# First products and gelus of 16 of 128 expert blocks moved behind the step that builds the routing weights

## The chip, the cores and the metric

The kernel runs on one core of one Trainium2 chip. The metric is device time in microseconds (us) of one execution, as the median of several runs. The engines are PE (TensorE, matrix products), DVE (VectorE), ACT (ScalarE), POOL (GpSimd) and SP (SyncE, which only issues transfers here). Each engine takes its instructions strictly in the order in which the program lists them.

## What is computed

One encoder layer runs on two groups of tokens, a prompt of 256 and a sample of 1024. The part that matters is its last one, a mixture of 16384 experts (PEER). For each token, 8 heads pick 16 experts each. A picked expert has a row of `peer_u` and a row of `peer_v`:

```
act = gelu(einsum('td,thkd->thk', zt, u)) * g      # zt: the normalised token, u: rows of peer_u, g: softmax of the picks
out = einsum('thk,thkd->td', act, ve)              # ve: the same experts' rows of peer_v
```

The result is added to the token and normalised once more.

## The kernel before, in words

A token's experts are worked out in one of two ways. In blocks of 128 tokens that **gather**, the picked rows are fetched one slot at a time by indirect transfers that POOL issues: `ug` (rows of `peer_u`, 512 KB for 128 tokens) is multiplied and summed by DVE at L940, and `vg` (rows of `peer_v`) goes either to PE at L976 (`v_steps`) or to DVE at L996 (`v_slots`, the last two blocks). Both share one ring of seven buffers. Six token blocks gather: two of the prompt and four of the sample. The other 512 tokens of the sample are **dense**: all 16384 experts are computed for them, in 128 expert blocks of 128 experts.

For the dense tokens the order of the work is this. `merge` picks experts; at its end `half` and `finish_picks` work out, for each of four dense chunks of 128 tokens, the picks' codes (DVE with some ACT work) and store them in `codes` (L911). `weights` then builds the routing weight of each expert for each token: `cs` loads the codes, PE makes indicators (L1034), ACT and DVE turn them into `ol` and `oh`, PE multiplies these (L1053), ACT copies the result to `gs` (L1054), and after every eighth of its 128 groups `gs` is stored in DRAM as `gd`. Last, `dense` takes the 128 expert blocks in groups of four. `first(b)` loads a block of `uT` (512 KB), splits it in a high and a low part (`uh` on ACT, `ul` on DVE), multiplies it with the tokens `zt` in 24 matmuls (L140 to L142 with `zth`, `ztl`), applies the gelu (ACT, L1080), multiplies with the weights `g`, loaded from `gd` for four blocks at a time, and splits the product into `ah` and `al`. `second(g)` loads eight pieces of `peer_v` (256 KB each), splits them into `vh` and `vl`, and does 96 matmuls for the four blocks.

The gathers of the sample's blocks run beside all of this: those of the first block beside the end of `merge`, those of the others beside `weights` and `dense`. In `v_steps` every fourth gathered `vg` is followed on PE by eight matmuls of L976, one **slot group** below; between two of them POOL issues four `vg` and four `ug`. A token block has 32 slot groups. The scheduler fixes the order of every engine when the program is built, so a slot group has a fixed place among PE's other matmuls. A block of 24 first products is called a **first block** below.

The pools that matter: `uraw`, `uh` and `ul` have two buffers each, `ge` two. Until the change, `weights` has five PSUM banks and `dense` three for its first products.

Of the kernel before, what the change touches and what calls it, by code (L numbers as in the profile page):

```python
# [12 lines left out]
F32 = mybir.dt.float32  # L13
# [5 lines left out]
AF = mybir.ActivationFunctionType  # L19
# [5 lines left out]
P = 128  # L25
D = 1024
KD = D // P
# [23 lines left out]
def encoder(ctx, tc, I, O, dbg=None):  # L51
    nc = tc.nc
# [3 lines left out]
    dram = ctx.enter_context(tc.tile_pool(name="dram", bufs=1, space=DRAM))  # L56
# [56 lines left out]
    qd_ = dram.tile([MH, 96, SS], F32, name="qd_")  # L113
    ND = 512
    gd = dram.tile([ND // TC, P, P * TC], F32, name="gd")
    codes = dram.tile([ND // P, 2, P, 4, P], BF16, name="codes")


    def split(pool, src, shape, name, bufs=None, eng=None):
        kw = {} if bufs is None else {"bufs": bufs}  # L120
        hi = pool.tile(shape, F32R, name=name + "h", tag=name + "h", **kw)
        lo = pool.tile(shape, F32R, name=name + "l", tag=name + "l", **kw)
        nc.scalar.copy(hi, src)  # L123
        (eng or nc.vector).tensor_tensor(lo, src, hi.bitcast(F32), op=OP.subtract)  # L124
        return hi, lo
# [10 lines left out]
    def mm(out, w, x, start, stop):  # L136
        if len(w) == 1:
            nc.tensor.matmul(out, w[0], x[0], start=start, stop=stop)  # L138
            return
        nc.tensor.matmul(out, w[0], x[0], start=start, stop=False)  # L140
        nc.tensor.matmul(out, w[0], x[1], start=False, stop=False)  # L141
        nc.tensor.matmul(out, w[1], x[0], start=False, stop=stop)  # L142
# [11 lines left out]
    def put(dst, src):  # L154

        if len(dst) == 1:
            nc.scalar.copy(dst[0], src)
        else:
            nc.scalar.copy(dst[0], src)
            nc.vector.tensor_tensor(dst[1], src, dst[0].bitcast(F32), op=OP.subtract)  # L160
# [764 lines left out]
    def ring(name):  # L925
        return pe_.tile([P, D], F32, name=name, tag="ring", bufs=RING)
# [75 lines left out]
    def final_gain():  # L1002
        gfin = ring("gfin")
        nc.sync.dma_start(gfin, I["norm_final"].partition_broadcast(P))
        return gfin

    def finish(y, sq, tt, gfin=None):
        gfin = final_gain() if gfin is None else gfin
        ss = pe_.tile([P, 1], F32, name="fss", tag="fss")
        nc.scalar.activation(out=sq, in_=y, func=AF.Square, accum_out=ss)  # L1010
        rs = pe_.tile([P, 1], F32, name="frs", tag="frs")
        rsqrt_small(pe_, rs, ss, 1.0 / D, [P, 1], "fin")
        nc.vector.scalar_tensor_tensor(out=y, in0=y, scalar=rs[:, 0:1], in1=gfin, op0=OP.mult, op1=OP.mult)
        nc.gpsimd.dma_start(O["y"][tt:tt + P], y)
# [43 lines left out]
    def load_split(pool, src, shape, name, bufs):  # L1058
        raw = pool.tile(shape, F32, name=name + "raw", tag=name + "raw", bufs=2)
        nc.sync.dma_start(raw, src)  # L1060
        return split(pool, raw, shape, name, bufs)

    def dense(routes, zt, acc, dp, up, bankS, bankV):

        nt = len(routes)
        nch = ND // TC
        held = {}
        a_of = {}

        def first(b):  # L1070
            u = load_split(up, I["uT"][b], [P, KD, P], "u", 2)
            if b % HB == 0:
                held["g"] = dp.tile([P, nch, HB, TC], F32, name="g", tag="g", bufs=2)
                nc.scalar.dma_start(held["g"].rearrange("p c h t -> p c (h t)"),
                                    gd[:, :, b * TC:(b + HB) * TC].rearrange("c p x -> p c x"))
            pm = bankS()
            for k in range(KD):
                mm(pm, [x[:, k] for x in u], [x[:, k] for x in zt], k == 0, k == KD - 1)
            ge = dp.tile([P, ND], F32, name="ge", tag="ge", bufs=2)
            nc.scalar.activation(out=ge, in_=pm, func=AF.Gelu)  # L1080
            gev = ge.rearrange("p (c t) -> p c t", t=TC)
            nc.vector.tensor_tensor(gev, gev, held["g"][:, :, b % HB], op=OP.mult)
            a_of[b] = (dp.tile([P, ND], F32R, name="ah", tag="ah", bufs=GE + 1),
                       dp.tile([P, ND], F32R, name="al", tag="al", bufs=GE + 1))
            put(a_of[b], ge)

        def second(g):
            for n in range(2):
                ns = slice(n * 512, (n + 1) * 512)
                vs = [load_split(dp, I["peer_v"][b * P:(b + 1) * P, ns], [P, 512], "v", 2 * GE)  # L1090
                      for b in range(g * GE, (g + 1) * GE)]
                for t in range(nt):
                    pm = bankV()
                    for i in range(GE):
                        mm(pm, [x[:, t * P:(t + 1) * P] for x in a_of[g * GE + i]], vs[i], i == 0, i == GE - 1)
                    nc.vector.tensor_tensor(acc[:, t, ns], pm, acc[:, t, ns], op=OP.add)  # L1096

        for t, r in enumerate(routes):
            nc.sync.dma_start(acc[:, t], x2d[r["tt"]:r["tt"] + P])
        first(0)  # L1100
        for g in range(P // GE):
            for b in range(g * GE + 1, (g + 1) * GE + 1):
                if b < P:
                    first(b)
            second(g)
        gfin = final_gain()
        for t, r in enumerate(routes):
            finish(acc[:, t], ring("sq"), r["tt"], gfin)
# [16 lines left out]
    def psum_pool(ctx, name, n, side):  # L1125
        pool = ctx.enter_context(tc.tile_pool(name=name, bufs=n, space=bass.MemoryType.PSUM, side=side))
        return lambda: pool.tile([P, 512], F32, name="pm", tag="pm")
# [94 lines left out]
    with ExitStack() as gctx:  # L1222
        zt = merge(s0, QG, SS - QG, ND // P, rs, wr, rp, psum_pool(gctx, "psC1", 5, "left"), cut=2, tbank=bankt, tctx=tctx)
    wrctx.close()
    with ExitStack() as gctx:
        bankG = psum_pool(gctx, "psG", 5, "left")
        gp = gctx.enter_context(tc.tile_pool(name="GW", bufs=1, side="left"))
        weights(rs[:ND // P], gp, bankG)
    up0 = ctx.enter_context(tc.tile_pool(name="DU0", bufs=1, side="right"))
    tctx.close()  # L1230
    rd, r1 = rs[:ND // P], rs[ND // P:]
    vp = ctx.enter_context(tc.tile_pool(name="VA", bufs=1, side="right"))
# [3 lines left out]
    acc = ctx.enter_context(tc.tile_pool(name="DA", bufs=1, side="left")).tile([P, ND // P, D], F32, name="acc")  # L1236
    up = ctx.enter_context(tc.tile_pool(name="DU", bufs=1, side="left"))
    dense(rd, zt, acc, up, up0, psum_pool(ctx, "psS", 3, "left"), psum_pool(ctx, "psV", 3, "left"))


# [75 lines left out]
```

## Time and profile before

| | |
|---|---|
| median of 3 runs | 4283.1 us (4270.11 to 4289.93) |
| the profiled execution | 4300.6 us, span of the trace 4298.8 us |
| mean granted clock of PE | 0.941 |
| busy share of PE, DVE, ACT, POOL | 88%, 75%, 36%, 42% |
| mean rate of the transfers | 294 GB/s |

The granted clock is a share of PE's full clock. PE's matmuls are pipelined, so their listed durations overlap; what one costs is read from the time between two starts. Busy time of PE is not PE at its peak. The profiled execution is 17.5 us above the median of the runs, and inside their scatter but for 11 us.

### The profile page before, as it was taken

To read this page: it belongs to the slowest core of one execution; us is meant where nothing else is said; L and a number is where in the kernel's file an instruction comes from. 1 tells how busy PE (TensorE), PEld (TensorE's weight loads), DVE (VectorE), ACT (ScalarE), POOL (GpSimd) and SP (SyncE) were. 2 spreads that over 40 slices of the span, in tenths; PEclk is the share of its full clock that TensorE was granted. 3 is DMA by queue.
4 is the path that set the end of the run, shared out by engine and by line. 5 is a ranking of instruction groups with operands and counts; after the bars stand their busy time and mean duration, and the time that the engine had idled before them with its cause. 6 is when DMAs were issued, how large, how long until landed. Compare 5 with 4: busy or idle time off the path is not lost.

```text
span 4298.8 us, 55005 instructions
## 1 busy us (share of the span) xinstructions
PE 3802.2 (88%) x18206; PEld 2734.5 (64%) x18206; DVE 3234.1 (75%) x8002; ACT 1559.9 (36%) x2600; POOL 1818.6 (42%) x1565
## 2 busy tenths in 40 slices
PE   6998999997777988877988489999999999899998
PEld 5777777775434753345644155677777877777786
DVE  4637988567988773986679985567668999999954
ACT  5555455454233214431201187522222222222232
POOL 0000644334444343774545512344446556666500
PEclk9999999998888999888999688999999999999999
DMA  5455899889999987998988847899999999999941
GB/s 160 123 183 152 324 344 343 315 305 319 318 311 313 323 312 272 328 339 326 334 293 285 292 181 292 325 322 339 334 333 356 339 358 362 365 364 346 326 140 64
DMA packets 508318, 1263.92 MB, mean 294 GB/s; under 512 B 49920, under 2 KB 203136, under 8 KB 505984
## 3 DMA queue, kind: packets, MB, share of 16 engines
q0 software_dynamic: 224352, 816.94, 52.9%
q1 hardware_dynamic: 197056, 354.05, 24.2%
q10 hardware_dynamic: 86624, 89.40, 6.1%
q8 instruction: 144, 2.36, 0.2%
q14 instruction: 142, 1.16, 0.1%
HBM read 1165.05 MB, written 95.16 MB: 293 GB/s over the span
## 4 chain that ended last, share of the span: by engine, by line
PE 55%; DMA 13%; DVE 12%; issue 12%; ACT 4%; POOL 2%; SPq 0%; another core or an unknown queue 0%; POOLq 0%; ACTq 0%; DVEq 0%
PE pm L140 12%; PE pm L141 11%; PE pm L142 11%; PE pm L138 7%; DMA vg<-peer_v,eit 5%; PE acc L976 5%; DVE ug L940 4%; DMA ug<-peer_u,ei 3%; PE pm L1053 3%; POOL ug L938 1%; PE pm L1034 1%; PE pm L437 1%; DVE vacc L996 1%; POOL vg L969 1%; PE pm L624 1%
## 5 line engine op out<-in xcount | busy, mean ns | idle before, releaser
L938 POOL DMA_INDIRECT ug<-peer_u,ei x768 | 908.9, 1184 | 800.8 <-DVE ug L940 334.2
L940 DVE SCALAR_TENSOR_TENSOR ug<-ug,zs 128x1024 f32<-128x1024 f32 x768 | 931.5, 1220 | 252.6 <-DMA ug<-peer_u,ei 189.3
L969 POOL DMA_INDIRECT vg<-peer_v,eit x512 | 540.7, 1056 | 752.8 <-DVE ug L940 308.9
L994 POOL DMA_INDIRECT vg<-peer_v,ei x256 | 354.7, 1385 | 207.0 <-DVE vacc L996 120.3
L141 PE MATMUL pm<-vl,ah 128*128 128x512 f32 x1024 | 405.1, 397 | 22.8 <-DVE vl L124 22.8
L140 PE MATMUL pm<-zth,uh 128*128 128x512 f32 x1024 | 406.3, 397 | 8.7 <-ACT ge L1080 6.0
L142 PE MATMUL pm<-zth,ul 128*128 128x512 f32 x1024 | 405.2, 396 | 0.0
L141 PE MATMUL pm<-ztl,uh 128*128 128x512 f32 x1024 | 404.8, 395 | 0.0
L976 PE MATMUL acc<-vg,zt 128*32 128x512 f32 x2048 | 284.6, 679 | 133.7 <-DMA vg<-peer_v,eit 132.8
L142 PE MATMUL pm<-vh,al 128*128 128x512 f32 x1024 | 400.6, 394 | 0.0
L140 PE MATMUL pm<-vh,ah 128*128 128x512 f32 x1024 | 374.9, 398 | 11.3 <-DVE acc L1096 5.5
L996 DVE SCALAR_TENSOR_TENSOR vacc<-vg,act,vacc 128x1024 f32<-128x1024 f32 x256 | 327.7, 1280 | 3.0 <-DMA vg<-peer_v,ei 0.9
L138 PE MATMUL pm<-xg,wraw 128*128 128x256 f32 (+1 forms) x1024 | 295.2, 441 | 4.1 <-DVE sr L855 4.1
L123 ACT CAST uh<-uraw 128x1024 fp32r<-128x1024 f32 x128 | 134.5, 1051 | 432.5 <-PE pm L141 413.2
L123 ACT CAST vh<-vraw 128x512 fp32r<-128x512 f32 x256 | 157.5, 618 | 352.0 <-DMA vraw<-peer_v 257.3
L140 PE MATMUL pm<-hh,wh 128*128 128x512 f32 x672 | 269.9, 402 | 5.0 <-ACT gt L240 3.0
L141 PE MATMUL pm<-hl,wh 128*128 128x512 f32 x672 | 268.3, 399 | 0.0
L142 PE MATMUL pm<-hh,wl 128*128 128x512 f32 x672 | 266.3, 396 | 0.0
L138 PEld LDWEIGHTS pm<-xg,wraw 128*128 128x128 f32 x1024 | 193.2, 194 | 80.6 <-issue 56.9
L141 PEld LDWEIGHTS pm<-vl,ah 128*128 128x128 f32 x1024 | 194.0, 189 | 75.1 <-DVE vl L124 31.5
L140 PEld LDWEIGHTS pm<-vh,ah 128*128 128x128 f32 x1024 | 194.1, 190 | 66.4 <-DVE acc L1096 14.1
L140 PEld LDWEIGHTS pm<-zth,uh 128*128 128x128 f32 x1024 | 192.2, 188 | 64.6 <-ACT ge L1080 11.4
(368 smaller groups left out, 7502.1 us busy)
## 6 DMA issues: line engine op xcount, KB each, us to landing
uraw<-uT SPq DMA_DIRECT2D x128, 512.0 KB
vraw<-peer_v SPq DMA_DIRECT2D x256, 256.0 KB
wraw<-wi SPq DMA_DIRECT2D x84, 512.0 KB
gd<-gs ACTq DMA_DIRECT2D x16, 2048.0 KB
g<-gd ACTq DMA_DIRECT2D x32, 1024.0 KB
wraw<-wq SPq DMA_DIRECT2D x48, 512.0 KB
wraw<-wo SPq DMA_DIRECT2D x24, 512.0 KB
ug<-peer_u,ei POOLq DMA_INDIRECT x768
```

The lines of the kernel that those rows point to most:

```text
L123: nc.scalar.copy(hi, src)
L138: nc.tensor.matmul(out, w[0], x[0], start=start, stop=stop)
L140: nc.tensor.matmul(out, w[0], x[0], start=start, stop=False)
L141: nc.tensor.matmul(out, w[0], x[1], start=False, stop=False)
L142: nc.tensor.matmul(out, w[1], x[0], start=False, stop=stop)
L938: nc.gpsimd.indirect_dma_start(out=ug, out_offset=None, in_=I["peer_u"], in_offset=bass.IndirectOffsetOnAxis(ap=ei[:, s:s + 1], axis=0))
L940: nc.vector.scalar_tensor_tensor(out=ug, in0=ug, scalar=1.0, in1=zs, op0=OP.mult, op1=OP.mult, accum_out=dots[:, s:s + 1])
L969: nc.gpsimd.indirect_dma_start(out=vg, out_offset=None, in_=I["peer_v"], in_offset=bass.IndirectOffsetOnAxis(ap=eit[:, t:t + 1], axis=0))
L976: nc.tensor.matmul(acc[g_ * 32:(g_ + 1) * 32, n * 512:(n + 1) * 512], zt[:, h, g_, i], v_[:, n * 512:(n + 1) * 512], start=b == 0 and i == ...
L994: nc.gpsimd.indirect_dma_start(out=vg, out_offset=None, in_=I["peer_v"], in_offset=bass.IndirectOffsetOnAxis(ap=ei[:, s:s + 1], axis=0))
L996: nc.vector.scalar_tensor_tensor(out=acc, in0=vg, scalar=act[:, s:s + 1], in1=acc, op0=OP.mult, op1=OP.add)
L1053: nc.tensor.matmul(pm[:, j * P:(j + 1) * P], ol[:, j], oh[:, j], start=True, stop=True)
```

## The change

The first products and gelus of expert blocks 0 to 15 are written in the code behind the loop of `weights`, and their results go to a new DRAM tensor `ged`, 256 KB a block, by a store that SP issues. In `dense`, `first(b)` loads `ge` from `ged` for these blocks, again by SP, and goes on as before. The pool `DU0` (`uraw`, `uh`, `ul`) is opened ahead of `weights`; `weights` has four PSUM banks, and the early blocks have one of their own.

```diff
+    EB = 16
+    ged = dram.tile([EB, P, ND], F32, name="ged")
...
+    def scores_u(b, zt, up, gp, bankS):
+
+        u = load_split(up, I["uT"][b], [P, KD, P], "u", 2)
+        pm = bankS()
+        for k in range(KD):
+            mm(pm, [x[:, k] for x in u], [x[:, k] for x in zt], k == 0, k == KD - 1)
+        ge = gp.tile([P, ND], F32, name="ge", tag="ge", bufs=2)
+        nc.scalar.activation(out=ge, in_=pm, func=AF.Gelu)
+        return ge
...
         def first(b):
-            u = load_split(up, I["uT"][b], [P, KD, P], "u", 2)
+            if b >= EB:
+                ge = scores_u(b, zt, up, dp, bankS)
+            else:
+                ge = dp.tile([P, ND], F32, name="ge", tag="ge", bufs=2)
+                nc.sync.dma_start(ge, ged[b])
             if b % HB == 0:
...
-            pm = bankS()
-            for k in range(KD):
-                mm(pm, [x[:, k] for x in u], [x[:, k] for x in zt], k == 0, k == KD - 1)
-            ge = dp.tile([P, ND], F32, name="ge", tag="ge", bufs=2)
-            nc.scalar.activation(out=ge, in_=pm, func=AF.Gelu)
...
+    up0 = ctx.enter_context(tc.tile_pool(name="DU0", bufs=1, side="right"))
     with ExitStack() as gctx:
-        bankG = psum_pool(gctx, "psG", 5, "left")
+        bankG = psum_pool(gctx, "psG", 4, "left")
+        bankE = psum_pool(gctx, "psE", 1, "left")
         gp = gctx.enter_context(tc.tile_pool(name="GW", bufs=1, side="left"))
+        egp = gctx.enter_context(tc.tile_pool(name="EG", bufs=1, side="left"))
         weights(rs[:ND // P], gp, bankG)
-    up0 = ctx.enter_context(tc.tile_pool(name="DU0", bufs=1, side="right"))
+        for b in range(EB):
+            nc.sync.dma_start(ged[b], scores_u(b, zt, up0, egp, bankE))
     tctx.close()
```

Where the instructions land is the scheduler's doing. On PE, before the change, the end of `merge` holds slot groups (L976) and the transposes of the picks' weights (L912), up to the first indicator matmul (L1034):

```order
L912 MATMUL pm<-ident,gw 128x128
L976 MATMUL acc<-vg,zt_3898 32x512 x8
L912 MATMUL pm<-ident,gw 128x128
L954 MATMUL acc<-ident,act 128x128
L1034 LDWEIGHTS cs
L1034 MATMUL pm<-cbk,cs 128x512
```

With the change the same place on PE reads, just ahead of the first indicators (line numbers grow by two, L1036 is the indicator; the rows are the last of the eighth early block, the indicators, and the first of the ninth):

```order
L142 MATMUL pm<-zth,uh 128x512
L143 MATMUL pm<-ztl,uh 128x512
L144 MATMUL pm<-zth,ul 128x512
L1036 LDWEIGHTS cs
L1036 MATMUL pm<-cbk,cs 128x512
```

Eight first blocks (192 matmuls) now stand between the slot groups and the first indicators; the other eight are spread among the first 17 of the 128 groups of `weights`, and nothing of them stands after that.

On ACT the picks' exponentials (L823, L825 with the change) and casts (`scr`) stood together before the change:

```order
L123 CAST uh<-uraw 128x1024 x2
L823 ACTIVATE gw<-gw,rt 128x64
L914 COPY w<-pm 128x128
L835 CAST scr<-ranki 128x1024
L835 CAST scr<-rankj 128x1024
L823 ACTIVATE gw<-gw,rt 128x64
L914 COPY w<-pm 128x128
```

With the change the splits `uh` and the gelus (L1072) of the early blocks stand between them, and tables are loaded at each turn from one function to the other:

```order
L825 ACTIVATE gw<-gw,rt 128x64
L837 CAST scr<-ranki 128x1024
L125 CAST uh<-uraw 128x1024
L1072 ACT_TABLE_LOAD
L1072 ACTIVATE ge<-pm 128x512
L916 COPY w<-pm 128x128
L837 CAST scr<-rankj 128x1024
L825 ACT_TABLE_LOAD
L825 ACTIVATE gw<-gw,rt 128x64
```

ACT has 12 table loads more in all, and all of them stand in this place.

On SP, before the change, the codes' stores and loads follow right on the first four `uraw`:

```order
L1060 DMA uraw<-uT 128x1024 x4
L911 DMA codes<-co 128x2x512
L1004 DMA gfin<-norm_final 128x1024
L933 DMA gffn<-norm_ffn 128x1024
L1028 DMA cs<-codes 64x2x128 x6
```

With the change a store of `ged` and a load of `uraw` alternate there, and the first store of codes stands behind five such stores (the rows from the fifth store on):

```order
L1244 DMA ged<-ge 128x512
L1062 DMA uraw<-uT 128x1024
L913 DMA codes<-co 128x2x512
L1244 DMA ged<-ge 128x512
L1006 DMA gfin<-norm_final 128x1024
L935 DMA gffn<-norm_ffn 128x1024
L1062 DMA uraw<-uT 128x1024
L1030 DMA cs<-codes 64x2x128 x4
```

Each store of `ged` waits on SP for its gelu, and what stands behind it on SP waits with it.

## Rows read from the trace of the kernel before

**Rows 1.** Stretches: PE, PEld, DVE, ACT, POOL busy (instructions), granted clock, DMA share, GB/s.
```profile
2436.34:2489.88 53.54, 13.06 (x54) 2.71 (x54) 49.74 (x261) 12.52 (x21) 23.77 (x24) 0.56 0.79 263
2489.88:2738.38 248.50, 234.51 (x1358) 148.10 (x1359) 169.33 (x459) 196.15 (x273) 50.64 (x52) 0.93 0.67 253
2738.38:2827.61 89.23, 87.22 (x412) 66.31 (x412) 47.02 (x70) 27.79 (x38) 35.28 (x32) 1.00 0.92 330
2827.61:2978.00 150.39, 150.39 (x710) 111.78 (x710) 103.41 (x164) 44.66 (x69) 70.26 (x64) 1.00 0.92 329
2978.00:3242.30 264.30, 262.47 (x1243) 193.66 (x1245) 172.76 (x267) 70.43 (x106) 123.34 (x112) 1.00 0.93 334
3242.30:4089.00 846.70, 806.74 (x3400) 638.59 (x3393) 801.30 (x1034) 235.11 (x352) 521.88 (x387) 0.99 0.97 351
4089.00:4281.50 192.50, 191.58 (x831) 155.47 (x829) 95.31 (x150) 59.55 (x92) 1.14 (x2) 1.00 0.32 99
```

**Rows 2.** PE in order of time at the end of merge: start, us, what, idle before.
```profile
2432.70 3.64 PE L976 MATMUL acc<-vg,zt 128*32 128x512 f32 x16 [14.91 <-DMA vg<-peer_v,eit]
...
2489.88 3.17 PE L1034 MATMUL pm<-cbk,cs 64*128 64x512 bf16 x7 [4.49 <-DMA cs<-codes]
```

**Rows 3.** The chain that ended last, 2250 to 2860: start, us, what.
```profile
2482.17 3.27 DMA codes<-co
2485.51 4.32 DMA cs<-codes
...
2602.39 1.85 PE acc L976 x16
...
2827.61 1.85 PE acc L976 x16
```

**Rows 4.** Tiles uraw and ge, whole run: ns min/median/max, first and last start.
```profile
L123 ACT CAST uh<-uraw x128: 1036/1052/1058, 2422.8 to 4247.6; 128x1024 fp32r<-128x1024 f32 x128
L124 DVE TENSOR_TENSOR ul<-uraw,uh x128: 1207/1221/1289, 2424.9 to 4248.6; 128x1024 fp32r<-128x1024 f32 x128
...
L1080 ACT ACTIVATE ge<-pm x128: 584/594/603, 2755.6 to 4259.7; 128x512 f32<-128x512 f32 x128
```

**Rows 5.** ACT in order of time, a table load and what follows it.
```profile
2486.97 1.28 ACT L823 ACT_TABLE_LOAD   x1
2488.27 0.35 ACT L823 ACTIVATE gw<-gw,rt 128x64 f32<-128x64 f32 x1
```

**Rows 6.** Transfers from 2742 to 3242: queues (packets, MB, share), then issues.
```profile
q0 software_dynamic: 29710, 108.14, 58.6%
q1 hardware_dynamic: 18032, 43.59, 24.4%
q10 hardware_dynamic: 24912, 14.68, 9.7%
...
vraw<-peer_v SPq DMA_DIRECT2D x86, 256.0 KB
uraw<-uT SPq DMA_DIRECT2D x41, 512.0 KB
g<-gd ACTq DMA_DIRECT2D x12, 1024.0 KB
...
vg<-peer_v,eit POOLq DMA_INDIRECT x102
ug<-peer_u,ei POOLq DMA_INDIRECT x101
```

**Rows 7.** Groups by line: busy, mean ns, idle before; PE from 2742, POOL 2742 to 3242.
```profile
L976 PE MATMUL acc<-vg,zt 128*32 128x512 f32 x416 | 50.0, 598 | 1.8 <-DMA vg<-peer_v,eit 1.8
...
L969 POOL DMA_INDIRECT vg<-peer_v,eit x102 | 116.0, 1137 | 152.6 <-DVE ug L940 123.7 <-issue 19.1 <-PE acc L976 7.3
```

**Rows 8.** Transfer rates: 2415 to 2490 in 40 slices; a stretch of 100 us.
```profile
GB/s 199 326 234 363 411 413 409 402 411 413 317 76 260 301 332 345 374 260 153 194 245 293 365 264 326 347 299 293 66 240 306 291 284 406 153 238 243 247 268 68
...
3700.00:3800.00 100.00, 90.68 (x379) 71.39 (x378) 94.91 (x152) 26.55 (x40) 65.97 (x52) 0.98 1.00 375
```

## The prediction

> **What bounds the kernel now.** I cut the span into stretches at the slot groups that matter [rows 1] and then asked each one who waits. I number the slot groups of the second gathered block of the sample from 0 (at 2602.39) to 31 (at 3242.3); group 9 is at 2827.61 [rows 3] and group 17 at about 2978. The reader is to see five stages.
>
> The gap, 2436.34 to 2489.88: PE finishes a slot group [rows 2] and has little to do until the first indicator, which waits for the codes' store and load (3.27 and 4.32 us, [rows 3]). PE is busy 13.06 of 53.54 us at a granted clock of 0.56, which lies near the lower of its two levels, 1.2 GHz; DVE is busy 49.74 us of it, with the picks. So DVE sets the end of the gap.
>
> The weights, to 2738.38 (end of slot group 5): PE is busy 234.51 of 248.50 us, clock 0.93, transfers only 0.67 [rows 1].
>
> The early dense stage, to 3242.30: PE is busy without a break at full clock, and the transfers take 0.92 to 0.93. PE never waits there for a gathered `vg` (1.8 us in all), but the gathers are not far ahead: of POOL's 152.6 us of waiting ahead of `vg`, 123.7 are for DVE to free a buffer and 7.3 for PE [rows 7].
>
> The late dense stage, to 4089: DVE busy 801.30 of 846.70 us, transfers 0.97, PE 806.74. The tail, to 4281.50, is PE alone [rows 1].
>
> So PE has room only in the gap, and a little in the weights.
>
> **The price of a matmul.** The stretch from 2827.61 to 2978 has no idle PE. Its 8 slot groups cost 1.85 us each [rows 3], 14.8 in all; the other 135.6 us are 585 matmuls by the order, 0.232 us each. A first block is 24 of them, 5.6 us; the 16 that are moved are 89 us.
>
> **Term 1, the gap.** Eight first blocks go here. PE's own floor: from 2436.34, 8 x 5.6 = 44.5, three slot groups at full clock 5.6, four transposes 2, and eight waits for the one PSUM bank at 0.9 (gelu 0.59 [rows 4], and 0.3 that I choose for the two handovers, which no row has alone) 7: 2495. But the first indicator waits for the picks, and these get longer: five `ul` of 1.22 us [rows 4] stand on DVE ahead of the first codes' store, 6.1, and DVE has hardly a hole; three table loads stand ahead of exponentials of the picks, 1.28 each [rows 5], 3.8; and the gap's 14.1 MB of transfers (263 GB/s) grow by 8 x (0.52 + 0.26) = 6.3 MB, which at the 351 GB/s of the late stage makes 58 us of 53.5, so 4.6. That is 14.5 us: the first indicator at 2504. Bounds: 2495 (PE alone), and 2523 if all ACT work of the eight blocks (8 x (1.05 + 0.59 + 1.28) = 23.4) and all `ul` (9.8) lie on the picks' chain. The sum is nearest to the instructions that the order puts ahead of the codes, so I keep 2504.
>
> In the trace a table load takes 1.28 us, and the exponential starts 0.02 us behind its end [rows 5]. The Trainium skill (ScalarE: Activation LUTs, What ACT_TABLE_LOAD costs) puts a drain of about 1.38 us beside the load, 2.66 us a switch. By that page the three would cost 8 us rather than 3.8; the row shows no such gap ahead of the exponential.
>
> **Term 2, the weights.** Before, 125.5 of the 128 groups took 248.50 - 6 x 1.85 = 237.4 us, 1.89 each with all waits; 128 take 242. With the change PE does, from the first indicator to slot group 9, these, 9 slot groups (16.7), 213 matmuls of first blocks (49.4), and eight bank waits, half of them covered by matmuls of the weights in between (3.6): 312 us, so group 9 is at 2816, 11.5 us earlier than now. By then PE has done 405 matmuls of the dense stage instead of 336: 69 x 0.232 = 16.0. Together the change is **27.5 us ahead** at group 9. Bounds: the eight blocks fill what PE loses now, 14 us of idle time and 7% of low clock, 16: 34 better with the bank waits gone; or every block waits a gelu and a table load in full, 15 worse.
>
> **Term 3, the stretch behind it.** From group 9 to 17 PE has by the order 347 matmuls instead of 585, almost all of them second products, because blocks 4 to 15 need no first products any more. PE could do it in 347 x 0.232 + 14.8 = 95 us. But the eight slot groups stand among them as before, about 45 matmuls apart instead of 73, and each needs its eight gathers; and the loads of `peer_v` are as many per second product as before, with `ged` (256 KB a block) on top. By the transfers from 2742 to 3242 [rows 6]: 58.6% of 500 us is 293 us for 205 gathers and like transfers of q0, 1.43 each; q1 2.8 us per MB, 0.73 per 256 KB; q10, the loads of `g`, 3.5 each. The stretch has 64 gathers (91.5), some 30 `vraw` and 14 `ge` (32.3), 3 `g` (10.4), 2 `uraw` (2.9): 137 us of all 16 engines' time, and at the share of 0.93 that the stage has now, **147 us**. Now it takes 150.4. So 3.4 us are won and 238 matmuls, 55.2 us, are not done: a loss of 51.8. What was hidden behind PE's first products comes to light: the transfers become the bound, and PE waits for `vg` at L978. Bounds: 49.3 MB at the 413 GB/s of the best slices [rows 8] take 119 us, 28 better; at the share of 0.79 that the gap had with the gathers running, 174, 27 worse.
>
> The stretch begins with the first `g`, which can be loaded only when the last `gd` is stored; PE has three first blocks ahead of that (17 us), where it now has more. I put nothing for it, since the gathers go on meanwhile and the transfers set the length.
>
> **The rest.** From group 17 to 31 PE has 1024 matmuls instead of 1001: it stays without idle time, and what it takes longer it has done more. The late stage has the same gathers and the same DVE work per block, and 846.7 us again; the tail is PE's. **Sum**: 51.8 - 27.5 = 24 us later, 4323 of the span against 4298.8. The profiled execution is 17.5 us above the median of the runs, and a difference of 24 us goes over: 4283.1 + 24 = **4307 us**, 0.6% slower. About 0.5%, 21 us, is what these runs can tell from no change.
>
> **Rivals.** *The weights' holes take the blocks* (4307 - 34 = 4273, not to be told from no change). For it: the indicators leave PE at a clock of 0.93 and idle 14 us. Against it: ACT is busy 196 of these 248 us and gets more.
>
> *The gathers keep up* and the stretch takes PE's 95 us: 4307 - 52 = 4255, faster. The place is group 9 to 17; it decides in favour below 102 us. For it: transfers have reached 413 GB/s in slices of 2 us, and a busy transfer's time holds waiting. Against it: 49.3 MB in 95 us is 519 GB/s, and no stretch of 100 us has more than 375 [rows 8].
>
> The Trainium skill (DMA: Bandwidth & Descriptors, Specifications) gives about 358 GB/s as a core's limit towards HBM; by that the stretch takes 138 us and the kernel 4298. The trace passes that figure, 375 GB/s over 100 us [rows 8], so it is no hard wall here, but the page would leave this rival no room.
>
> *SP's queue holds the picks up.* The first codes' store stands behind five stores of `ged`, the loads of `cs` behind six, and each waits for a gelu that waits for PE. If that sets the pace, the first indicator is at 2523 or later (+19), and the eight blocks inside the weights pay their table loads and gelus in full (+15): 4341. It decides from 2520 on. For it: all of this is in program order on SP and ACT; against it: a block takes PE 5.6 us, and five are done before the codes are due.
>
> **How the numbers follow.** The forecast 0.45 (of it 0.33 beyond 0.5%, the rest within), the holes 0.25 (0.03 of it faster), the gathers 0.12, SP's queue 0.18. So slower 0.51, same 0.34, faster 0.15. The range leaves out the gathers' case below and the far end of SP's case above: 4268 to 4346; the forecast's own is 4290 to 4325.
>
> **What would show it.** Right: PE busy at full clock in the gap, first indicator near 2504; slot group 9 near 2816; from there eight slot groups about 18 us apart, PE waiting some 50 us for `vg`, transfers at 0.93 or more; group 31 within 15 us of 3242; the late stage as long as now. Wrong: slot groups 12 to 14 us apart there, or the first indicator past 2520, or a late stage that is shorter by tens of us because the gathers end earlier than PE's order expects.

## The result and the profile after

The changed kernel takes 4317.1 us (median of 5 runs, 4313.8 to 4332.3), the kernel before 4277.2 us on the same chip (5 runs, 4265.7 to 4289.9). The ratio is 1.0096 with a 95% interval of [1.0077, 1.0115]: about 40 us slower. The forecast was 24 us slower, 4307, with a range of 4268 to 4346.

The stretches of the changed kernel, by the columns of [rows 1]; the first runs, as there, from the end of the landmark slot group (the last one ahead of the gap) to the first indicator, the second to the issue of the last store of `gd`, the third line shown from slot group 10 to 11, the fourth from 11 to 17, the fifth from 17 to 31:

```profile
2420.05:2489.31 69.26, 56.48 (x246) 39.99 (x246) 64.82 (x313) 32.19 (x43) 26.39 (x24) 0.94 0.82 283
2489.31:2796.93 307.62, 285.19 (x1620) 182.14 (x1619) 191.97 (x454) 223.29 (x300) 82.64 (x84) 0.96 0.76 279
...
2818.02:2849.09 31.07, 11.40 (x47) 7.21 (x47) 13.36 (x21) 5.70 (x9) 10.22 (x9) 0.73 0.86 296
2849.09:2960.54 111.45, 87.51 (x363) 56.35 (x363) 71.61 (x121) 20.43 (x34) 51.44 (x48) 0.86 0.95 341
2960.54:3227.07 266.53, 266.03 (x1250) 196.83 (x1249) 176.29 (x277) 72.75 (x112) 122.27 (x111) 1.00 0.92 330
3227.07:4089.00 861.93, 824.51 (x3467) 656.70 (x3467) 811.84 (x1045) 242.21 (x368) 512.86 (x387) 0.98 0.96 348
4089.00:4300.00 211.00, 210.67 (x915) 171.41 (x914) 101.59 (x159) 63.24 (x95) 0.65 (x2) 1.00 0.32 100
```

The gap is filled: PE is busy 56.48 of 69.26 us at a granted clock of 0.94, where it was busy 13.06 of 53.54 at 0.56. The gap is 16 us longer, and PE does 192 matmuls of the dense stage in it, 44.5 us by the prediction's price. Behind the weights there is a new hole: 31 us with 11.40 of PE, then 111 us with 87.51 at a clock of 0.86, where [rows 1] had PE busy without a break at 1.00. From slot group 17 on PE is busy again as before.

PE in order of time there (start, us, what, idle before):

```profile
2489.31 1.03 PE L1036 MATMUL pm<-cbk,cs 64*128 64x512 bf16 x4
...
2802.02 1.92 PE L978 MATMUL acc<-vg,zt 128*32 128x512 f32 x16
...
2818.02 1.92 PE L978 MATMUL acc<-vg,zt 128*32 128x512 f32 x16 [1.97 <-DMA vg<-peer_v,eit]
2837.47 1.65 PE L142 MATMUL pm<-vh,ah 128*128 128x512 f32 x3 [17.53 <-ACT vh L125]
...
2846.10 0.98 PE L142 MATMUL pm<-vh,ah 128*128 128x512 f32 x3 [2.14 <-ACT ah L161]
...
2849.09 1.92 PE L978 MATMUL acc<-vg,zt 128*32 128x512 f32 x16
...
2960.54 1.93 PE L978 MATMUL acc<-vg,zt 128*32 128x512 f32 x16
```

**The account.** Two profiled executions of one program differ by up to 16 us upstream of the change, so I time everything from one landmark, the last slot group ahead of the gap (2432.70 in [rows 2], 2416.4 in the changed kernel), and count what PE has done. *Behind* is the time from there, less the same in the execution before, less 0.232 us for each first or second product of the dense stage done more than there. Negative is ahead. These numbers are worked out from the traces' records and from the order of the matmuls, us:

```
                       first      slot    slot    slot    slot    end of    last
                       indicator  gr. 9   gr. 11  gr. 17  gr. 31  gathers   matmul
changed kernel          -28.8     -25.2    -1.0   +36.9   +36.2   +36.8     +36.2
before, run again        +0.8     -15.9   -15.9   -15.5   -16.4   -16.1     -17.0
```

In the changed kernel 25 us are won ahead of slot group 9, 24 are lost from 9 to 11, 38 more from 11 to 17, and nothing changes afterwards. The second row (run `e5_before_again`, below) shows how far an execution of the same program strays: 16 us, all of them in the step that builds the weights, and it keeps within 1.5 us everywhere behind it. So, as far as one pair of executions tells, what stands behind slot group 9 can be read to some 1.5 us, the lead at slot group 9 only to some 16.

### The profile page after: what moved, and what is told of

It reads as the page before. It is cut to its first block, busy times and chain, and to the rows that moved or that the text cites. A ratio compares the mean times of both kernels' runs of the same rounds, so it can differ in the third digit from the quotient of the medians.

```text
span 4318.7 us, 55171 instructions
## 1 busy us (share of the span) xinstructions
PE 3809.2 (88%) x18206; PEld 2738.6 (63%) x18206; DVE 3232.2 (75%) x8002; ACT 1576.9 (37%) x2612; POOL 1807.0 (42%) x1565
## 4 chain that ended last, share of the span: by engine, by line
PE 36%; issue 11%; DMA 10%; DVE 6%; POOL 3%; ACT 1%; POOLq 0%; DVEq 0%; SPq 0%; ACTq 0%
PE pm L142 8%; PE pm L143 8%; PE pm L144 7%; DMA vg<-peer_v,eit 4%; DMA ug<-peer_u,ei 4%; PE pm L140 4%; PE acc L978 4%; PE pm L1055 2%; DVE ug L942 2%; POOL ug L940 2%; PE pm L1036 1%; PE pm L626 1%; DMA vraw<-peer_v 1%; PE pm L620 1%; POOL vg L971 1%
## 5 line engine op out<-in xcount | busy, mean ns | idle before, releaser
L940 POOL DMA_INDIRECT ug<-peer_u,ei x768 | 925.2, 1205 | 800.4 <-DVE ug L942 321.7
L971 POOL DMA_INDIRECT vg<-peer_v,eit x512 | 530.9, 1037 | 747.5 <-DVE ug L942 301.4
L996 POOL DMA_INDIRECT vg<-peer_v,ei x256 | 336.7, 1315 | 229.7 <-DVE vacc L998 164.3
```

What stands on the lines that cost most here:

```text
L940: nc.gpsimd.indirect_dma_start(out=ug, out_offset=None, in_=I["peer_u"], in_offset=bass.IndirectOffsetOnAxis(ap=ei[:, s:s + 1], axis=0))
L971: nc.gpsimd.indirect_dma_start(out=vg, out_offset=None, in_=I["peer_v"], in_offset=bass.IndirectOffsetOnAxis(ap=eit[:, t:t + 1], axis=0))
L996: nc.gpsimd.indirect_dma_start(out=vg, out_offset=None, in_=I["peer_v"], in_offset=bass.IndirectOffsetOnAxis(ap=ei[:, s:s + 1], axis=0))
```

## What the hole is made of

**The start.** ACT, DVE and POOL in order of time around slot groups 10 and 11 (the line at 2810.89 is the second of the two loads that the line above it sums up):

```profile
2796.90 0.33 ACTq L1058 DMA_DIRECT2D gd<-gs  x1
...
2810.49 14.23 ACTq L1090 DMA_DIRECT2D g<-gd  x2
2810.89 13.83 ACTq L1090 DMA_DIRECT2D g<-gd  x1
2824.84 1.04 ACT L125 CAST uh<-uraw 128x1024 fp32r<-128x1024 f32 x1 [13.54 <-DMA vraw<-peer_v]
2836.28 0.62 ACT L161 CAST ah<-ge 128x512 fp32r<-128x512 f32 x1 [10.40 <-DVE ge L1093]
```

```profile
2825.91 1.23 DVE L126 TENSOR_TENSOR ul<-uraw,uh 128x1024 fp32r<-128x1024 f32 x1 [8.81 <-ACT uh L125]
2835.56 0.69 DVE L1093 TENSOR_TENSOR ge<-ge,g 128x512 f32<-128x512 f32 x1 [8.42 <-DMA g<-gd]
```

```profile
2823.92 0.94 POOL L940 DMA_INDIRECT ug<-peer_u,ei  x1 [0.31 <-issue]
2841.63 1.67 POOL L971 DMA_INDIRECT vg<-peer_v,eit  x1 [16.77 <-DVE ug L942]
```

Read them from the bottom. POOL issues no gather for 16.8 us because DVE frees no buffer. DVE is idle for 17 us, in two pieces: it waits for `uh`, then for the first `g`, and the next four `ug` products stand behind `ge * g` in its order. `uh` is late because ACT's order has the issue of two loads of `g` ahead of it, 14.23 us, of which the second, for blocks 4 to 7, takes 13.83. The name that the trace gives for ACT's own 13.54 us (`vraw`) is not the cause: ACT's queue was in the issue of `g` meanwhile.

The wait that ends last is that for the first `g`: DVE's `ge * g` goes on at 2835.56, then ACT's `ah` at 2836.28, `vh` behind it, and PE's second products at 2837.47, after 17.53 us. That load was issued at 2810.49 and is used 25.1 us later. In the execution before, the first product with `g` stood at 2769.33, 15.8 us behind the issue at 2753.49, and did not wait for it. The queues of the transfers (packets, MB, share of 16 engines), from 2814 to 2832 and then from 2832 to 2837; q10 has the loads of `g`, q0 the gathers:

```profile
q0 software_dynamic: 1173, 4.26, 58.1%
q10 hardware_dynamic: 1963, 1.00, 18.5%
...
q10 hardware_dynamic: 2119, 1.07, 71.0%
q0 software_dynamic: 17, 0.05, 2.3%
```

Of the 2.1 MB of the two loads, half was moved in the 18 us in which gathers went on beside them, and half in 5 us when next to none were left. These rows read as if the gathers held up the first `g`, and the first `g`, by way of DVE, then the gathers; no run tests the first half of that.

The first `g` cannot be loaded before the last `gd` is stored; that store is issued at 2796.90, and the two loads are out 27.8 us later. In the execution before they were out 16.0 us after the store (the issue took 4.46 us there). With other blocks early (`e1`, `e4` below) the issue takes about as long, 12.87 and 11.42 us, but PE has first products to do meanwhile, and the start costs it 4 and 2 us by the account. Why the second issue takes so long is not shown.

**The pace behind it.** The waits of PE from slot group 9 to 17 (total, times, longest), and ACT's longest from 11 to 17:

```profile
PE pm L142 <- ACT vh L125: 22.8, 5, 17.5
PE pm L142 <- DVE acc L1107: 8.2, 2, 6.2
PE pm L143 <- DVE vl L126: 6.9, 4, 2.9
PE acc L978 <- DMA vg<-peer_v,eit: 5.5, 2, 3.5
PE pm L142 <- ACT ah L161: 2.1, 1, 2.1
```

```profile
ACT vh L125 <- DMA vraw<-peer_v: 60.2, 16, 8.5
```

PE hardly waits for a gathered `vg` (5.5 us). It waits for the halves of `peer_v`'s pieces, and ACT, which makes the high ones, has waited 60.2 of 112 us for the pieces themselves. From 11 to 17 PE's waits sum to 24 us. The 266 matmuls and six slot groups there cost 72.8 us at the prediction's prices, and PE was busy 87.51: so of the 38 us lost, some 24 are waits and some 14 stand beside the lower granted clock of 0.86. The transfers from slot group 9 to 17 (queue, packets, MB, share of 16 engines; then issues with the median us to landing):

```profile
q0 software_dynamic: 9192, 33.46, 57.1%
q1 hardware_dynamic: 6618, 12.84, 22.6%
q10 hardware_dynamic: 10386, 6.06, 12.4%
...
vraw<-peer_v SPq DMA_DIRECT2D x28, 256.0 KB, 5.5
g<-gd ACTq DMA_DIRECT2D x5, 1024.0 KB, 17.3
ge<-ged SPq DMA_DIRECT2D x16, 256.0 KB, 7.3
```

And three pieces of the chain that ended last:

```profile
2877.10 6.53 DMA ge<-ged
...
2894.61 9.47 DMA vg<-peer_v,eit
...
2928.43 11.36 DMA vraw<-peer_v
```

All three kinds of transfer take their turn on the chain, at a DMA share of 0.95. But a piece of `peer_v` lands 5.5 us after its issue in the median; much of its lateness lies ahead of the issue. SP, which issues the pieces, waits from 11 to 17 for `vl`, whose making frees one of the two buffers of `vraw`, and for `al`, whose making frees one of the two of `ge` (total, times, longest):

```profile
SPq L1062 <- DVE vl L126: 56.3, 20, 7.4
...
SPq L1087 <- DVE al L162: 16.6, 10, 8.5
```

In the execution before SP waited for `vl` too, 66.7 of 150 us in the same stretch, while PE had other work. So there are two candidates for the pace: the rate at which everything is moved, and the round of a piece through its two buffers.

## The experiments

Where an experiment changes the choice of early blocks, `EARLY` names them. The kernel before ran beside each set on the same chip: 4298.4 us (24 runs) beside `e1` to `e4`, 4275.4 (12 runs) beside `e5` to `e8`, 4296.9 (10 runs) beside `e9` to `e11`. The ratios are taken on one chip; the accounts all compare with the one execution before of [rows 1], which took 4300.6 us on the first chip. The two theories at the start: the loss lies in the stretch that has lost its first products and is one of place (**stretch**), or the early work costs about as much wherever its blocks are taken from (**rival**).

### Other blocks early: e1 to e4

```diff
-    EB = 16
+    EARLY = list(range(112, 128))    # e1; e2: range(120, 128), e3: range(4, 128, 8), e4: range(16, 32)
...
-            if b >= EB:
+            if b not in EARLY:
...
-        for b in range(EB):
-            nc.sync.dma_start(ged[b], scores_u(b, zt, up0, egp, bankE))
+        for i, b in enumerate(EARLY):
+            nc.sync.dma_start(ged[i], scores_u(b, zt, up0, egp, bankE))
```

`e1_last16`:

> The early blocks are the last sixteen (112 to 127) instead of the first sixteen; what is done behind the weights' steps is the same. The stretch theory (early work wins some 41 us by slot group 9, and the stretch of second products beside the gathers loses some 62) expects that the loss goes, since the last blocks stand in the tail, where the transfers are at a share of 0.32: 4317 - 62 = 4255 us, 20 to 30 below the kernel before. The rival (the early work itself costs more than it saves, by its stores, reloads, table loads and one PSUM bank) expects the time of the change, 4317 us, give or take 10.

`e2_last8`:

> Eight early blocks, the last eight (120 to 127). By the order they all stand in the gap ahead of the first indicator, none among the weights' groups. The stretch theory expects what the gap gives, 8 x 5.6 = 45 us, and no loss: about 4277 - 40 = 4237 us, and if the eight blocks among the weights are neutral, the same as with sixteen. The rival expects half of the change's loss, 4297 us.

`e3_spread16`:

> Sixteen early blocks, every eighth (4, 12, ... 124), so that no two groups of second products follow each other without first products. The stretch theory expects that most of the loss goes, but ten of the blocks still lie beside the gathers, where PE has no room to gain from 2742 to 3242: 4255 to 4275 us. The rival expects 4317 us.

`e4_mid16`:

> The early blocks are 16 to 31: the stretch of second products is there, but later, and the dense stage begins with first products as before, so that PE does not wait for the first g (17.5 us in the profile of the change). If the stretch costs by its transfers, only this start goes: about 4300 us. If the start is all of the loss, it comes near the kernel with the last sixteen, 4255 to 4270 us. The rival of the early work expects 4317 us.

Measured (us, ratio to before with its interval), and the account of the profiled executions:

```
                     median    ratio                     slot gr. 9   11      17      20      26      31     end of    last
                                                                                                            gathers   matmul
e1_last16            4296.9    1.0000 [0.9979, 1.0022]     -16.1    -12.4   -12.4   -12.4   -12.5   -14.3   -12.7      -5.2
e2_last8             4294.7    1.0003 [0.9983, 1.0023]     -19.6    -19.6   -19.5   -19.6   -19.7   -21.6   -13.0      -8.5
e3_spread16          4313.2    1.0049 [1.0030, 1.0068]     -25.3    -22.3   -18.0   -18.1   -18.3   -20.1   +15.8     +14.8
e4_mid16             4319.6    1.0084 [1.0046, 1.0121]     -29.0    -26.8   -26.8   -27.0    +5.6    +3.7    +7.5      +6.6
```

The loss goes where the blocks go. With blocks 16 to 31 early, slot groups 9 to 20 are as fast as before and 33 us are lost from 20 to 26, where these blocks' first products had stood; the start costs 2. With the last 16, the last 8 or every eighth block there is no such stretch. That is the stretch theory's account. The rival, put as ratios, expects 1.0096 from `e1`, `e3` and `e4` and half of that from `e2`; the intervals of `e1`, `e2` and `e3` exclude it. That of `e4` does not, and there it is the account that decides: the loss has moved. (The execution of `e4` that the account shows is its fastest, 4300.9 us, 19 below the median.) But my numbers for the gain were too high: I expected 4255 and 4237 from `e1` and `e2` where before has 4277, and neither can be told from no change; `e3`, expected at 4255 to 4275, is slower than before. I had taken the early gain as 41 us, and 16 of these were the upstream scatter described above; and part of it is given back in the weights (below) and in the end. So early work has a price of its own, if not the rival's. `e3` shows another place where first products are not worth their 5.6 us: 36 us are lost from slot group 31 to the end of the gathers, where PE does not set the length alone: DVE is busy 801 of 847 us there, and the transfers stand at 0.97 [rows 1]; by the count of matmuls nine of its 16 early blocks, 44 to 108, fall into that stage, 50 us by PE's price.

### The same program again, and one PSUM bank less: e5 and e6

`e5` is the kernel before, unchanged. `e6` is the kernel before with four banks for the weights and no early blocks:

```diff
-        bankG = psum_pool(gctx, "psG", 5, "left")
+        bankG = psum_pool(gctx, "psG", 4, "left")
```

> The kernel before, unchanged, once more with a profile. It says how far two executions of one kernel differ from the end of the slot group at the gap (92) on, and so what the comparison by slot groups can tell. Every theory expects the same stages within 3 us: first indicator 57 us behind group 92, last group of the weights 308, group 105 at 395, group 127 at 808, last matmul at 1848.

> The kernel before with four PSUM banks instead of five in the weights' step, and no early blocks. In the run with the last eight blocks the weights' step took 263 us instead of 251, though none of the early blocks stands in it. If the bank that was taken away is the reason, this kernel's weights take 260 us or more and its time is some 10 us above the kernel before. If the reason is another (the gathers' place, the clock), it is the time before, 251 us for the weights.

`e5` took 4267.6 us in its one run. `e6` took 4288.9 (9 runs), ratio 1.0045 [1.0026, 1.0063]: the bank by itself costs 19 us, 11 to 27 by the interval. Their weights, from the first indicator to the last product, by the columns of [rows 1], and the wait of PE's products for ACT's copy to `gs`, first of `e5`:

```profile
2474.64:2709.25 234.61, 227.59 (x1377) 144.96 (x1378) 168.80 (x459) 196.41 (x275) 51.95 (x54) 0.97 0.71 268
```

```profile
PE pm L1053 <- ACT gs L1054: 1.0, 3, 0.6
```

and of `e6`:

```profile
2479.86:2734.25 254.39, 235.53 (x1393) 146.50 (x1394) 174.52 (x472) 198.45 (x277) 60.69 (x63) 0.95 0.71 265
```

```profile
PE pm L1053 <- ACT gs L1054: 9.7, 17, 0.6
```

With four banks PE waits 17 times for a bank that ACT has not yet emptied, where it waited 3 times, and in the execution of [rows 1] twice (0.8 us). With the indicators' waits for the same copies the sums are 11.2 us in `e6`, 1.5 in `e5` and 6.4 there. That execution took 250.7 us for the step, only 4 less than `e6`, so the 19 us rest on the medians and not on one pair of traces. I had expected 260 us or more. The Trainium skill (Perfetto Trace Analysis, Matmuls) says that independent groups of matmuls should take turns in different banks, so that the emptying of one lies beside the next group's matmuls; these rows agree.

### Fewer loads in the stretch: e7, e8, e9

All three are the changed kernel with loads left out. In `e7` one load of gelus serves the 16 blocks; in `e8` also half of `peer_v`'s pieces are left out for them; in `e9` four pieces, the first halves of blocks 0 to 3, serve all 16 (my expectation says eight). The matmuls and the gathers stay; the splits of the pieces that are not loaded go with the loads.

```diff
-                nc.sync.dma_start(ge, ged[b])
+                if b == 0:
+                    held["e"] = dp.tile([P, ND], F32, name="ge0")
+                    nc.sync.dma_start(held["e"], ged[0])
...
+                if n == 0 or g >= EB // GE:             # e8; in e9: if g == 0 and n == 0 or g >= EB // GE
                     vs = [load_split(dp, I["peer_v"][b * P:(b + 1) * P, ns], [P, 512], "v", 2 * GE)
```

> The change with one load of stored gelus instead of sixteen: block 0's gelus are used for all sixteen early blocks (the output is not the reference's). It takes some 3.9 MB, 11 us of all transfer engines' time by the price of the prediction, out of the stretch of second products. If the stretch is bound by the bytes moved, groups 107 to 113 (111 us in the change, for 266 matmuls and six slot groups, 73 us on PE) get some 8 to 10 us shorter. If it is bound by the gathers' own round (issue, landing, DVE, free buffer), they stay at 18 us a group. In both, what is lost at the start of the dense stage (22 us up to group 107, waiting for g) stays.

> As the one before, and the first sixteen blocks' second products use the loaded first half of peer_v for both halves (the second halves are neither loaded nor split for these blocks; the output is not the reference's). That takes another 4.2 MB, 12 us, and 11 us of DVE out of the stretch. Bound by bytes: groups 107 to 113 take some 85 to 93 us instead of 111. Bound by the gathers' own round: 105 us or more.

> For the first 16 expert blocks one load of gelus and one set of eight pieces of peer_v serve all blocks (so the output is not the reference's); the gathers beside them stay. The place is the six intervals between the slot groups that the prediction calls 11 and 17, 111 us in the changed kernel, 106 with one load of gelus, 103 with half of peer_v as well. If the transfers' bytes set this pace, only eight gathers (8 x 1.43) and a share of g are left for an interval, 13 to 14 us at a share of 0.93; PE's own work by the order is then longer (57 matmuls and a slot group, 15 us), so the six take 90 us and PE has no idle time. Rival, the gathers' own round (POOL's issue, the buffers that DVE frees, landing) takes 17 to 18 us whatever else is moved: 103 to 110 us, with PE waiting for vg or for what DVE gives out behind its ug products. The first interval behind the last store of weights (the start) is not touched by either: it should still cost about 20 us.

One run each: 4322.8, 4288.4, 4298.1 us. Slot group 11 to 17, columns of [rows 1]; of `e7`:

```profile
2858.20:2964.70 106.50, 86.98 (x382) 56.30 (x382) 70.12 (x120) 22.61 (x38) 51.42 (x48) 0.94 0.90 315
```

of `e8`:

```profile
2849.00:2952.30 103.30, 99.27 (x465) 71.39 (x464) 70.83 (x121) 20.21 (x35) 49.22 (x48) 0.98 0.91 315
```

and of `e9`, with PE's wait for `vg` there:

```profile
2871.20:2969.00 97.80, 92.62 (x440) 66.65 (x439) 63.15 (x107) 11.53 (x19) 50.18 (x48) 0.98 0.89 306
```

```profile
PE acc L978 <- DMA vg<-peer_v,eit: 1.5, 1, 1.5
```

```
                     slot gr. 9   slot gr. 11   slot gr. 17   lost 9 to 11   lost 11 to 17
changed kernel         -25.2          -1.0         +36.9           24             38
e7_one_ge              -24.6          +2.4         +31.9           27             30
e8_one_ge_half_v       -30.6          -4.9          +1.2           26              6
e9_gathers_alone       -23.8          +1.8          +8.6           26              7
```

By length none of the three met a number of its expectation. Lengths mislead here, since the scheduler put more matmuls between the slot groups once loads were gone (PE's busy time grows from 88 to 99 us); the account corrects for that. The loads of gelus are 8 of the 38 us; with half of `peer_v`'s loads gone as well, 32 of 38 are. In `e9` the last five intervals take 78.1 us, 15.6 each, PE's own work in them by the order is 75.1, and PE waits 1.5 us for `vg`: so the gathers can keep to 15.6 us a slot group when little but `g` is moved beside them. A round of their own of 17 to 18 us, the rival of `e9`, falls. The gathers' own limit is not shown, only that it is not above 15.6. And a high share does not show by itself that the transfers bind: it is still 0.89 in `e9`, where PE hardly waits for them. The start costs 24 to 27 us in all four and does not care for these loads, as it should if it hangs on the first `g`.

What these runs do not part: how much of `vraw`'s lateness is the transfers' rate, how much its place on SP's queue behind loads of `ge` that wait for a buffer, and how much the round through its own two buffers. `e7` takes the first two away at once; `e8` and `e9` take away, with the loads, the splits that free these buffers. No run has a third buffer.

### Eight blocks ahead of the weights: e10 and e11

If the bank is what costs in the weights and a run of blocks without first products is what costs behind them, then eight blocks that fill the gap, take turns in the weights' own five banks, and are taken from places where PE sets the pace should win. The blocks are written ahead of the weights:

```diff
-        bankG = psum_pool(gctx, "psG", 4, "left")
-        bankE = psum_pool(gctx, "psE", 1, "left")
+        bankG = psum_pool(gctx, "psG", 5, "left")
...
+        for i, b in enumerate(EARLY):
+            nc.sync.dma_start(ged[i], scores_u(b, zt, up0, egp, bankG))
         weights(rs[:ND // P], gp, bankG)
```

`e10` has `EARLY = list(range(120, 128))`, `e11` has `[8, 16, 24, 32, 112, 116, 120, 124]`.

> Only the last eight blocks (120 to 127) are early, they are written ahead of the weights and take turns in the weights' five banks, so none of them stands among the weights' groups and no bank is given away. If the lent bank was what ate the gap's 29 us in the run with the last eight blocks behind the weights (the run of before with four banks lost 13 to 19), the gain of the gap is kept: 25 to 29 us ahead at slot group 9 within the scatter of the clock in the weights' step, 12 or so lost in the late stage and the tail as in that run, the kernel about 4258 to 4264 where before has 4277, ratio 0.995 to 0.997. Rival: the loss in the weights' step comes from the work around it (ACT, DVE, tables), not from the bank: ratio 1.000.

> As the run with the last eight blocks ahead of the weights, but the early blocks are 8, 16, 24, 32 (one for each of four groups in the stage where PE has no idle time) and 112, 116, 120, 124 (one for each of four groups in PE's tail). If first products are worth their 5.6 us wherever PE sets the pace, and the loss of the last eight came from taking too many from one place, 25 to 29 us are kept to the end: ratio 0.993 to 0.995. Rival: what is gained ahead of the late stage is lost in it, since DVE and the gathers set its length: then only the four blocks of the tail are won, ratio 0.997 to 1.000.

```
                     median    ratio                     first ind.  slot gr. 9   17      31     end of    last
                                                                                                 gathers   matmul
e10_ahead8           4285.5    0.9969 [0.9951, 0.9986]    -35.9       -36.9     -36.2   -38.0    -22.9     -19.7
e11_ahead8_mix       4265.1    0.9923 [0.9902, 0.9944]    -32.4       -33.3     -33.5   -34.8    -37.0     -37.7
```

`e11` is faster than both kernels: 32 us below before (4 runs beside 10), and 74 us, by the two ratios, below the changed kernel. Its stretches: the last 55 us of the gap, the weights, slot group 9 to 17, the tail:

```profile
2443.97:2498.97 55.00, 44.59 (x214) 31.36 (x213) 53.88 (x248) 29.49 (x40) 20.77 (x18) 0.95 0.93 315
2498.97:2746.51 247.54, 233.22 (x1378) 147.77 (x1378) 164.84 (x425) 196.91 (x275) 58.60 (x58) 0.94 0.70 259
2829.20:2982.90 153.70, 153.70 (x724) 114.37 (x723) 108.19 (x171) 44.53 (x69) 67.73 (x65) 1.00 0.94 336
...
4089.00:4240.00 151.00, 150.90 (x657) 122.77 (x656) 79.81 (x136) 45.84 (x73) 1.14 (x2) 1.00 0.31 100
```

The gap is as full as with the change, the weights take 248 us, between the 251 and 235 of the two executions of the kernel before, rather than the 263 that `e2` needed with four banks, and slot groups 9 to 17 have no idle PE at all. `e10` keeps the same lead to slot group 31 and then loses 15 before the gathers end, 3 behind it; `e11`, with four of its blocks taken from the early dense stage and only every fourth from the tail, loses nothing. So the rival of `e11`, that a lead from ahead of the late stage is lost in it, falls for `e11`; `e10` loses 15 of its 38 us in that very stage, and why is not shown.

## Why the prediction was right, and where it was off

**Term 1, the gap: right.** The first indicator was put 71.3 us behind the landmark (2504 - 2432.7); it is at 72.9, the eight blocks done. The lead there is 28.8. The table loads take 1.28 us, and the splits, exponentials and gelus behind those in the gap begin 0.01 to 0.02 us after their end, as in [rows 5]: no more was to be paid for them.

**Term 2, the weights: right in its sum, not in its reason.** Slot group 9 was put at 383.3 us behind the landmark, 27.5 ahead; it is at 385.6, 25.2 ahead. I priced the bank of the early blocks but not the bank that the weights lose. `e6` prices that at 19 us. That the sum came out nonetheless is in part luck: the execution before that I summed against was slow in this very step (250.7 us where `e5` took 234.6 at a clock of 0.97), and against `e5` the lead is 9.3 us.

**Term 3, the stretch: the right mechanism in the main, one part put at nothing.** Slot group 9 to 17 was to take 147 us and took 158.5, 330 GB/s over it. Of the 11.5 us that are missing, 10 lie ahead of slot group 11 (47.1 us for two slot groups, where 147 / 8 gives 36.8), and 1 behind it (111.4 for six, where I had 110.3). So the price by the transfers was good to 1% for these six, and the step that failed is "I put nothing for it, since the gathers go on meanwhile". They stop for 16.8 us, because the `ug` products that free their buffers stand behind `ge * g` on DVE, and `ge * g` waits for the first `g`; and PE, which has second products next in its order, waits 17.53 us for the same load. I had looked at PE's first blocks as cover for that load and not at DVE's order.

The sum shows the same step in another way. I counted 3 loads of `g` in the stretch, and five are issued in it: now that the weights end only at slot group 9, the first two fall there. Queue q10 has 12.4% of 159 us, 19.7 us of all engines' time, where I had 10.4; at 0.93 that is 10 us more. The other queues come to 127 us, as forecast. From slot group 9 to 11 the share was 0.87 and not 0.93, which is 3 of the 10 us; the rest is what was moved there beyond my count.

I also said that PE would wait some 50 us for `vg`. It waits 5.5; lateness reaches PE through `vh`, `vl` and the banks of the second products, and some 14 us through the lower clock, for which I had no term. That the loads set the pace was right, its last link was wrong. `e7` and `e8` show that 32 of the 38 us go with the loads and their splits; that it is their rate, as I priced it, rather than the round through two buffers is not shown, and the 1% may be in part luck.

The rivals: the gathers that keep up with PE's 95 us would have needed 12 us a slot group and have 18.6. By the Trainium skill (DMA: Bandwidth & Descriptors, Specifications), with about 358 GB/s, the stretch as I counted it takes 138 us, and with the 52.4 MB that the three queues moved 146; its mean was 330, so that figure was not reached there, and the share of 0.93 priced it better. SP's queue did not hold up the picks: the first indicator is on time. The weights' holes did not take more than forecast.

**The rest: right.** From slot group 17 to the last matmul the account stays between +36 and +39. The late stage neither gave anything back nor took more.

**The sum.** +36.2 by the account where 24.3 was forecast: 2.3 more from the lead, 11.5 from the stretch, 1.2 less because the same stretch took 151.6 us before (I had 150.4), 0.7 less from what lies behind. The medians, 40 us apart with 33 to 49 by the interval, agree with the account; against the execution of `e5` it would be 53, and the medians lie between the two.

## What to carry to other kernels

Work that is taken out of a stage is worth its time only where its engine sets the pace, and a stage with transfers at 0.92 can have other work hidden behind the first: ask what will set the pace once it is thinned, and take the work from many places rather than from one, as `e11` does with one block in eight of the early dense stage and one in four of the tail. A buffer or a bank that is lent to the moved work is a cost of the move: try the lending alone. And where a load starts a stage, follow the waiting instruction on every in-order engine, since what stands behind it (here the products that free the gathers' buffers) is what gets late.

## What was not expected of the hardware

The same program took 250.7 us and 234.6 us for the same step, the weights. The first 80 us of it are alike in both; then 40 us of the execution before, and the same 40 of `e5`, by the columns of [rows 1]:

```profile
2569.88:2609.88 40.00, 35.71 (x209) 22.66 (x209) 29.43 (x70) 30.76 (x42) 14.76 (x16) 0.91 0.78 281
```

```profile
2554.64:2594.64 40.00, 39.68 (x250) 25.39 (x250) 34.64 (x82) 37.55 (x52) 15.96 (x17) 1.00 0.94 337
```

The first holds one wait of PE of 4.0 us for a bank, the second none, and the clock is 0.91 against 1.00. Over the step PE is idle 14.0 and 7.0 us, so 7 of the 16 us are waits and 9 stand beside the lower clock (0.93 against 0.97). A lead of 10 us in such a step cannot be read from one profile.

In the hole PE's granted clock was 0.73 and then 0.86, means over its two levels of 1.2 and 2.4 GHz, though PE's waits from slot group 11 to 17 sum to 24 of 111 us; in the stretch before the change, without waits, it was 1.00.
